# A branch over overflow code laid out in line, with a prefetch hint for TensorE, in a two-layer transformer trunk

## The chip, the cores and the metric

The kernel runs on one core of one Trainium2 chip. The metric is the device time of one execution in microseconds (us), as the median over several runs. The engines are TensorE (PE; its weight loads are PEld), VectorE (DVE), ScalarE (ACT), GpSimd (POOL) and SyncE (SP, which issues the DMAs here). Each engine has a sequencer that reads its own list of instructions; where an engine's name ends in q (PEldq, DVEq, SPq) the row is about the sequencer's own instructions, such as branches and DMA issues.

## The reference

A decoder trunk of two layers over 256 tokens of width 1024: in each, three parallel token mixers with a gated merge, then a layer of 16 experts with top-2 routing, each followed by a layer norm. What matters here is the expert layer:

```python
def moe_ffn(h, router_w, router_b, w1, w3, w2):
    hf = h.reshape(B * S, D)
    aff = jax.nn.sigmoid((hf @ router_w).astype(jnp.float32))
    ...
    combine = jnp.einsum('tk,tke->te', gate, jax.nn.one_hot(eidx, N_EXPERTS, dtype=jnp.float32)).astype(h.dtype)
    y = jnp.zeros_like(hf)
    for e in range(N_EXPERTS):
        y = y + combine[:, e:e + 1] * ((jax.nn.silu(hf @ w1[e]) * (hf @ w3[e])) @ w2[e])
    return y.reshape(B, S, D)
```

Every token goes to two of the 16 experts; w1 and w3 are 1024x512 and w2 is 512x1024 for each expert, in float32.

## The kernel before, in words

All weights are streamed from HBM in tiles of 1 MB (`wt`), each by one DMA that SP issues as soon as a buffer is free (`load`, L100). A layer runs its mixers first and then the experts.

The experts are taken in 8 pairs, p = 0 to 7, with room for CAP = 64 tokens for each expert. For one pair TensorE multiplies the gathered tokens `xe` with w1 and w3 (`up`, matmul L1557: 64 matmuls over 8 weight tiles), VectorE and ScalarE make the gated hidden value (`hidden`, L1567 to L1569), TensorE transposes it (`turn`, L1575), and multiplies it with w2 (`down`, L1600: 32 matmuls over 4 weight tiles). `combine` (L1515 in layer 0, L1520 in layer 1) adds the result, weighted, to the sums `z` or `y`. The order of the blocks on TensorE is written out by hand: `block()` issues each behind the one before it (the list `PEQ`). From p = 1 on the down-projection of pair p - 1 runs behind the up-projection of pair p; at p = 3 and p = 7 the pair's own down-projection follows at once.

An expert may be given more than 64 tokens. For that case there is `overflow()` (L1449 to L1497), once in each layer, behind the combine of pair 3. It loads the largest count of any expert into a register of every engine (`values_load`, L1452) and branches on it (`tc.If`, L1453). The body is four nested loops (L1468) that compute the experts' products over all 256 tokens for those beyond 64. With these inputs no expert has more than 64 tokens, so the body never runs: every engine goes from L1453 to whatever follows the body, on TensorE the up-projection of pair 4.

How the two ways out of L1453 are laid out in the instruction lists is set by the argument `preferred_fallthrough_block`. Before, it is False: behind the conditional branch stands the block for "no overflow", which holds a semaphore instruction and an unconditional branch that jumps over the overflow code.

```python
over = nc.values_load(mxi[0:1, 0:1], min_val=0, max_val=S)
with tc.If(over > CAP, preferred_fallthrough_block=False):
```

Of the kernel before, what the change touches and what calls it, by code (L numbers as in the profile page):

```python
# [25 lines left out]
CAP = 64  # L26
# [43 lines left out]
def trunk(ctx, tc, x, consts, pcol, rowv, gb, wfm, wng, wdv, wmla, wcmp, wcmp2, wu, wbr, wout, rw, mw1, mw3, mw2, out):  # L70
# [252 lines left out]
    def ln_cols(i, c):  # L323
        g0, b0 = PC_LN + 16 * i, PC_LN + 16 * i + 8
        return pc[:, g0 + c:g0 + c + 1], pc[:, b0 + c:b0 + c + 1]
# [1008 lines left out]
    def moe(l, R):  # L1334
# [93 lines left out]
        def affine():  # L1428
            w = load_gb(mh, 1 + 2 * l, "gt1", nc.sync)
            for j, op in enumerate((ALU.mult, ALU.add)):  # L1430
                for t in range(2):
                    V.tensor_tensor(out=res[:, t], in0=res[:, t], in1=w[:, j * D:j * D + D], op=op)
# [16 lines left out]
        def overflow():  # L1449
            V.tensor_scalar(wov, rks, float(CAP), None, op0=ALU.is_gt)  # L1450
            V.tensor_mul(wov, wov, cb)
            over = nc.values_load(mxi[0:1, 0:1], min_val=0, max_val=S)  # L1452
            with tc.If(over > CAP, preferred_fallthrough_block=False):  # L1453
                hx = mx[0].tile([P, 4, S], F32, name="hx", tag="xe0")
                hy = [gp.tile([P, 2, S], F32, name="hy", tag="yh") for _ in range(2)]
                hT = [hx[:, k] for k in range(4)] + [hy[k // 2][:, k % 2] for k in range(4)]
                for k in range(KD):
                    ps = pf.tile([P, S], F32, name="pt")
                    for t in range(2):
                        for j, src in enumerate((hhi, hlo)):  # L1460
                            T.matmul(ps, src(t, k)[:, 0], idb[:, P - P * t:3 * P - P * t],
                                     start=(t == 0 and j == 0), stop=(t == 1 and j == 1))
                    g, b = ln_cols(1 + 2 * l, k)
                    V.tensor_scalar(hT[k], ps, g, b, op0=ALU.mult, op1=ALU.add)
                up_w = [src[l].rearrange("q e p (k j h f c) -> q e p k j h f c", k=2, j=2, h=2, f=2) for src in (mw1, mw3)]
                down_w = mw2[l].rearrange("q c h p (f j o) -> q c h p f j o", f=2, j=2)
                wv = wov.rearrange("p t (q j) -> p t q j", j=2)
                with tc.For_i(0, E // 2, 1) as q, tc.For_i(0, 2, 1) as j, tc.For_i(0, 2, 1) as h, tc.For_i(0, 2, 1) as f:  # L1468
                    wc = gp.tile([P, 2], F32, name="wc")
                    V.tensor_copy(wc, wv[:, :, ds(q, 1), ds(j, 1)].rearrange("p t o a -> p (t o a)"))  # L1470
                    gf = gp.tile([P, S], F32, name="gf", tag="g")
                    pp = []
                    for src in up_w:
                        ps = pf.tile([P, S], F32, name="pt")
                        for e in range(4):
                            w = gp.tile([P, 2, P], F32, name="fa", tag="yl")
                            G.dma_start(w, src[ds(q, 1), e, :, :, ds(j, 1), ds(h, 1), ds(f, 1)].rearrange(
                                "a p k b d g c -> (a b d g p) k c"))
                            for k in range(2):
                                T.matmul(ps, w[:, k], hT[2 * e + k], start=(e == 0 and k == 0), stop=(e == 3 and k == 1))  # L1480
                        pp.append(ps)
                    A.activation(gf, pp[0], AF.Tanh, scale=0.5)
                    V.scalar_tensor_tensor(gf, gf, 1.0, pp[0], op0=ALU.add, op1=ALU.mult)
                    V.scalar_tensor_tensor(gf, gf, 0.5, pp[1], op0=ALU.mult, op1=ALU.mult)
                    for c in range(2):
                        w2 = gp.tile([P, 512], F32, name="fc", tag="yl")
                        G.dma_start(w2, down_w[ds(q, 1), c, ds(h, 1), :, ds(f, 1), ds(j, 1)].rearrange("a g p b d o -> (a g b d p) o"))
                        for t in range(2):
                            ps = pf.tile([P, 512], F32, name="pt")
                            T.matmul(ps, gf[:, t * P:(t + 1) * P], w2, start=True, stop=True)  # L1490
                            tm = gp.tile([P, 512], F32, name="tm", tag="g")
                            V.tensor_scalar(tm, ps, wc[:, t:t + 1], None, op0=ALU.mult)
                            if last:
                                T.matmul(ya[t][c], ident, tm, start=False, stop=False, skip_group_check=True)
                            for k in () if last else range(4):
                                T.matmul(ya[2 * c + k // 2][:, k % 2, t * P:(t + 1) * P], tm[:, k * P:(k + 1) * P], ident,
                                         start=False, stop=False, skip_group_check=True)  # L1497
# [48 lines left out]
        def block(f, *a):  # L1546
            with tc.issue_after(PEQ[-1]) if PEQ else nullcontext():
                i = f(*a)
            PEQ.append(getattr(i, "ins", i))
# [15 lines left out]
        def hidden(p, h1, h3):  # L1565
            g = gp.tile([P, FF], F32, name="g")
            A.activation(g, h1, AF.Tanh, scale=0.5)  # L1567
            V.scalar_tensor_tensor(g, g, 1.0, h1, op0=ALU.add, op1=ALU.mult)  # L1568
            V.scalar_tensor_tensor(g, g, wsl[:, p:p + 1], h3, op0=ALU.mult, op1=ALU.mult)  # L1569
            return g  # L1570
# [45 lines left out]
        for p in range(8):  # L1616
            hs = [pf.tile([P, FF], F32, name="pt") for _ in range(2)]
            for nm, hh in zip(("w1", "w3"), hs):
                block(up, p, nm, hh)
            if p == 0:  # L1620
                lent.close()
                mx.append(right.enter_context(tc.tile_pool(name="mx2", bufs=1, side="right", reuse_waits="tile")))
                gp = right.enter_context(tc.tile_pool(name="gp", bufs=2, side="right", reuse_waits="tile"))
                block(slot_weights, 0)
            g = hidden(p, *hs)
            if p in (0, 4):
                block(gather, p // 2 + 1)
                block(slot_weights, p // 2 + 1)
                block(slots_T, p)
                block(turn, p, g)  # L1630
                if p == 4 and last:
                    affine()
                continue
            block(down, p - 1)
            block(turn, p, g)
            block(slots_T, p)
            if p == 2:
                block(gather, 2)
                block(slot_weights, 2)
            if p == 7 and not last:  # L1640
                pool, tag = X0["zf"] = ST.take()
                Z["zf"] = pool.tile([P, KD, S], F32, name="zf", tag=tag)
                for k in range(KD):
                    block(residual, k)
            for c in range(2):
                block(combine, p - 1, c)
            if p in (3, 7):
                block(down, p)
            if p == 3:
                for c in range(2):  # L1650
                    block(combine, 3, c)
                overflow()
                PEQ.clear()
# [45 lines left out]
    for l in range(L):  # L1699
        rt, z, zf = moe(l, mixer(l, rt, z, zf))  # L1700
# [128 lines left out]
```

## Time and profile before

| | us |
|---|---|
| median of 3 runs | 1056.8 (1055.84 to 1057.39) |
| the profiled execution | 1058.08 |
| its span in the trace | 1056.4 |
| TensorE busy | 1012.6 (96% of the span) |
| VectorE busy | 533.9 (51%) |
| ScalarE busy | 424.0 (40%) |
| GpSimd busy | 31.8 (3%) |
| mean granted TensorE clock | 0.98 of full speed |

The span is what the rows below are timed in: their starts count from its beginning. The profiled execution's own time is 1.7 us longer than its span, and 1.3 us longer than the median of the three runs shown. Busy time counts the engine's own operations; branches, semaphore instructions and DMA issues are not counted in it.

### The profile page before, as it was taken

What the parts mean: (1) busy time and instruction counts of PE and PEld (TensorE: products, weight loads), DVE (VectorE), ACT (ScalarE), POOL (GpSimd) and SP (SyncE); (2) the same over time, 40 slices, a digit from 0 to 9 for tenths busy, and PEclk for the clock granted to TensorE, in tenths of its full rate; (3) what the DMA queues carried; (4) which work ended last, traced back from release to release, by engine and by line L of the source; (5) the groups of instructions that cost most, each with busy time, mean ns of one, the idle gap of its engine ahead of it and who ended that gap; (6) DMA issues with size and microseconds to landing.
All of it is one profiled execution on the core that took longest, in us unless ns stands there. A gap on an engine that the chain in (4) does not pass through costs nothing. (4 is left out here: it accounts for less than half of the span.)

```text
span 1056.4 us, 16800 instructions
## 1 busy us (share of the span) xinstructions
PE 1012.6 (96%) x6498; PEld 711.9 (67%) x6498; DVE 533.9 (51%) x1493; ACT 424.0 (40%) x991; POOL 31.8 (3%) x46
## 2 busy tenths in 40 slices
PE   8999999999999997999999999999999999979994
PEld 7888988999864343433587888799998544424332
DVE  7745778785762121211285558777777422102315
ACT  6563777555321021100465537855553221101111
POOL 0300000000000000000002001000000000000001
PEclk9999999999999998999989999999999999989997
DMA  9664335448777999999846534335497789999992
GB/s 356 253 231 150 121 121 180 164 157 358 297 272 317 421 421 420 420 421 420 294 176 218 187 125 157 145 135 181 162 381 282 284 327 421 421 419 420 420 420 92
DMA packets 45546, 294.91 MB, mean 279 GB/s; under 512 B 5137, under 2 KB 7953, under 8 KB 11793
## 3 DMA queue, kind: packets, MB, share of 16 engines
q1 hardware_dynamic: 44880, 291.51, 70.5%
q10 hardware_dynamic: 576, 2.24, 0.6%
q8 instruction: 53, 0.87, 0.3%
q14 instruction: 37, 0.30, 0.1%
HBM read 292.68 MB, written 1.05 MB: 278 GB/s over the span
## 5 line engine op out<-in xcount | busy, mean ns | idle before, releaser
L1557 PE MATMUL pt<-wt,xe 128*64 128x512 f32 x1024 | 229.0, 604 | 12.7 <-issue 12.6
L371 DVE TENSOR_TENSOR wlo<-wt,whi 128x1024 fp32r<-128x1024 f32 (+4 forms) x146 | 167.5, 1149 | 83.1 <-ACT whi L370 77.0
L370 ACT CAST whi<-wt 128x1024 fp32r<-128x1024 f32 (+4 forms) x146 | 143.8, 987 | 148.3 <-PE acc L376 106.2
L1557 PEld LDWEIGHTS pt<-wt,xe 128*64 128x64 f32 x1024 | 73.4, 139 | 153.5 <-issue 149.2
L375 PE MATMUL acc<-hi,whi 128*128 128x256 f32 x576 | 165.3, 288 | 1.7 <-ACT whi L370 0.8
L377 PE MATMUL acc<-hi,wlo 128*128 128x256 f32 x576 | 164.0, 286 | 0.9 <-DVE wlo L371 0.9
L376 PE MATMUL acc<-lo,whi 128*128 128x256 f32 x576 | 162.4, 282 | 0.0
L1600 PE MATMUL pt<-wt,gT 128*64 128x512 f32 (+1 forms) x544 | 113.7, 568 | 0.0
L375 PEld LDWEIGHTS acc<-hi,whi 128*128 128x128 f32 x576 | 108.2, 188 | 7.9 <-issue 3.9
L377 PEld LDWEIGHTS acc<-hi,wlo 128*128 128x128 f32 x576 | 108.3, 188 | 4.3 <-DVE wlo L371 2.1
L376 PEld LDWEIGHTS acc<-lo,whi 128*128 128x128 f32 x576 | 108.7, 189 | 0.3 <-DVE lo L339 0.2
L1609 ACT CAST yh<-pt 128x512 fp32r<-128x512 f32 (+1 forms) x34 | 19.1, 561 | 184.0 <-PE pt L1600 184.0
L1600 PEld LDWEIGHTS pt<-wt,gT 128*64 128x64 f32 x544 | 38.8, 137 | 70.3 <-issue 66.1
L1568 DVE SCALAR_TENSOR_TENSOR g<-g,pt 128x512 f32<-128x512 f32 x16 | 11.0, 686 | 136.7 <-ACT g L1567 136.7
L1610 DVE TENSOR_TENSOR yl<-pt,yh 128x512 fp32r<-128x512 f32 (+1 forms) x34 | 22.4, 660 | 105.8 <-ACT yh L1609 103.1
L1567 ACT ACTIVATE g<-pt 128x512 f32<-128x512 f32 x16 | 9.6, 597 | 130.5 <-PE pt L1557 130.5
L375 PE MATMUL acc<-ob,whi 128*128 128x256 f32 x192 | 56.8, 296 | 1.1 <-DVE gt L892 0.8
L376 PE MATMUL acc<-ob,whi 128*128 128x256 f32 x192 | 54.2, 282 | 0.0
L377 PE MATMUL acc<-ob,wlo 128*128 128x256 f32 x192 | 54.1, 284 | 0.0
L1569 DVE SCALAR_TENSOR_TENSOR g<-g,wsl,pt 128x512 f32<-128x512 f32 x16 | 11.9, 747 | 69.0 <-PE pt L1557 69.0
L1382 ACT ACTIVATE xe<-pt,pc 128x128 f32<-128x128 f32 x60 | 24.2, 454 | 55.8 <-PE pt L1324 53.9
L659 DVE COPY ts<-pt 128x384 f32<-128x384 f32 x56 | 30.6, 553 | 30.7 <-PE pt L628 30.6
(399 smaller groups left out, 1773.4 us busy)
## 6 DMA issues: line engine op xcount, KB each, us to landing
wt<-in_mw SPq DMA_DIRECT2D x190, 1024.0 KB, 15.6
wt<-in_wfm SPq DMA_DIRECT2D x38, 1024.0 KB, 4.9
wt<-in_wbr SPq DMA_DIRECT2D x12, 1024.0 KB, 4.8
wt<-in_wcmp SPq DMA_DIRECT2D x8, 1024.0 KB, 6.2
wt<-in_wout SPq DMA_DIRECT2D x8, 1024.0 KB, 8.2
wt<-in_wdv SPq DMA_DIRECT2D x4, 1024.0 KB, 6.4
wt<-in_wmla SPq DMA_DIRECT2D x4, 832.0 KB, 5.2
wt<-in_wng SPq DMA_DIRECT2D x4, 560.0 KB, 10.6
```

The costliest lines, as they stand in the source:

```text
L370: X["hi"] = A.copy(hi, src).ins
L371: X["lo"] = V.tensor_sub(lo, src, hi.bitcast(F32)).ins
L375: T.matmul(ps, a[0], b[0], start=start, stop=False)
L376: T.matmul(ps, a[0], b[1], start=False, stop=False)
L377: return T.matmul(ps, a[1], b[0], start=False, stop=stop)
L659: X["ts"] = V.tensor_copy(ts, pt).ins
L1382: A.activation(x[:, k], pj, AF.Identity, bias=bb, scale=g)
L1557: i = T.matmul(hh[64 * j:64 * j + 64], xe[p][:, 2 * h + k, j * CAP:(j + 1) * CAP], wt[:, c0:c0 + FF], start=(h == 0 and k == 0), stop=(h = ...
L1569: V.scalar_tensor_tensor(g, g, wsl[:, p:p + 1], h3, op0=ALU.mult, op1=ALU.mult)
L1600: i = T.matmul(v[64 * j:64 * j + 64], gT[:, 2 * h + f, 64 * j:64 * j + 64], w2t[:, c0 + ks[0] * P:c0 + ks[1] * P], start=(h == 0 and f == ...
L1609: X0["yh"] = A.copy(yh[:, d], v).ins
L1610: V.tensor_sub(yl[:, d], v, yh[:, d].bitcast(F32))
```

## The change

It has two parts. The branch of L1453 is laid out the other way: the overflow code now follows the conditional branch directly, and the branch itself, taken, jumps over it. And ahead of the last down-projection before that branch, at p == 3, the program asks for a branch hint on TensorE that marks this branch, by its label, as likely taken. Both happen once in each layer.

```diff
-            with tc.If(over > CAP, preferred_fallthrough_block=False):
+            with tc.If(over > CAP, preferred_fallthrough_block=True, label="ov"):
...
             for c in range(2):
                 block(combine, p - 1, c)
+            if p == 3:
+                tc.mark_branch_hint_location('ov', 'LikelyTaken', engines=[mybir.EngineType.PE])
             if p in (3, 7):
                 block(down, p)
             if p == 3:
```

Two lines are added ahead of L1646, so later lines count two more in the changed kernel (L1825 becomes L1827).

TensorE's list around the branch in layer 0, where L1461 is the first matmul of the overflow code, reads:

```order
@@ -1877,5 +1878,4 @@
 L1452 TENSOR_LOAD mxi
 L1453 COMPARE_AND_BRANCH
-L1453 UNCONDITIONAL_BRANCH
 L1461 MATMUL pt<-idb,yh 128x256
 L1461 MATMUL pt<-idb,yl 128x256
```

The unconditional branch that stood between the conditional one and the overflow code is gone from there.

At the other end of the overflow code of layer 0, where its loops (L1468) close and the up-projection of pair 4 (L1557) begins, TensorE's list reads:

```order
@@ -1947,4 +1947,6 @@
 L1468 COMPARE_AND_BRANCH
 L1468 UNCONDITIONAL_BRANCH
+L1453 UNCONDITIONAL_BRANCH
+L1827 BRANCH_PREFETCH_HINT
 L1557 MATMUL pt<-wt,xe 64x512 x32
 L1324 MATMUL pt<-SS,yh 128x256
```

The "no overflow" block's branch now stands behind the overflow code, where it jumps to the next instruction and so has nothing to skip. Behind it stands a hint, ahead of everything else that TensorE does up to the next branch: it is the one for layer 1.

The hint for layer 0 stands at the start of TensorE's whole list, ahead of the warm-up matmuls on `junk`:

```order
@@ -1,4 +1,5 @@
-L1825 UNCONDITIONAL_BRANCH
-L1686 MATMUL pt<-junk 128x256 x3
+L1827 UNCONDITIONAL_BRANCH
+L1827 BRANCH_PREFETCH_HINT
+L1688 MATMUL pt<-junk 128x256 x3
 L291 MATMUL pt<-idf,r 128x128 x12
 L964 MATMUL acc<-z,gl 128x258 x10
```

So neither hint stands where the source line does, ahead of the last down-projection: the scheduler has moved both to the head of the straight piece of code that ends in the branch. Apart from these rows TensorE's list is the same as before, row for row. On the other engines the same unconditional branch moves behind the overflow code, and nothing else changes; they get no hint.

## Rows read from the trace of the kernel before

**Rows 1.** Busy time of each engine, whole span: us, share, instructions.
```profile
PE 1012.6 (96%) x6498; PEld 711.9 (67%) x6498; DVE 533.9 (51%) x1493; ACT 424.0 (40%) x991; POOL 31.8 (3%) x46
```

**Rows 2.** TensorE's waits, whole span: line waited for: us in total, times, longest.
```profile
PE pt L1557 <- issue: 12.6, 2, 6.4
PE acc L964 <- DVE z L298: 2.3, 2, 1.8
```

**Rows 3.** Chain that ended last, 930 to 1030 us: start us, us, what.
```profile
933.31 6.08 issue
939.39 16.88 PE pt L1557 x64
...
961.35 13.88 PE pt L1557 x64
...
975.23 6.87 PE pt L1600 x32
```

**Rows 4.** Line L1453, layer 0: engine op xcount: ns min/median/max, first to last start.
```profile
L1453 DVEq COMPARE_BRANCH  x2: 51/56/60, 412.6 to 412.8; - x2
L1453 PEldq COMPARE_BRANCH  x2: 98/3076/6053, 413.3 to 413.8; - x2
L1453 SPq COMPARE_BRANCH  x2: 38/46/53, 414.8 to 414.9; - x2
```

**Rows 5.** Line L1453, layer 1, the same columns.
```profile
L1453 PEldq COMPARE_BRANCH  x2: 81/2954/5827, 932.9 to 933.4; - x2
```

**Rows 6.** Timeline of TensorE: start, us, instruction xcount, [idle before <- releaser].
```profile
413.37 0.28 PE L1515 MATMUL z<-CT,yl 128*128 128x256 f32 x1
420.06 15.43 PE L1557 MATMUL pt<-wt,xe 128*64 128x512 f32 x64 [6.41 <-issue]
...
961.28 13.95 PE L1557 MATMUL pt<-wt,xe 128*64 128x512 f32 x64
```

**Rows 7.** Windows: us, busy PE PEld DVE ACT POOL, PEclk, DMA share, GB/s.
```profile
420.00:423.30 3.30, 3.24 (x9) 1.12 (x11) 0.00 (x0) 0.00 (x0) 0.00 (x0) 0.53 1.04 427
939.30:943.00 3.70, 3.61 (x10) 1.28 (x12) 0.00 (x0) 0.00 (x0) 0.00 (x0) 0.50 1.02 418
943.00:946.00 3.00, 3.00 (x12) 0.93 (x10) 0.00 (x0) 0.00 (x0) 0.00 (x0) 0.61 0.99 410
946.00:950.00 4.00, 4.00 (x20) 1.38 (x18) 0.00 (x0) 0.57 (x1) 0.00 (x0) 1.00 1.01 420
```

**Rows 8.** DMA queues: whole span, then 384 to 413, then 413.8 to 420: packets, MB, share.
```profile
q8 instruction: 53, 0.87, 0.3%
...
q8 instruction: 1, 0.02, 0.2%
...
q8 instruction: 1, 0.02, 1.1%
```

**Rows 9.** Timeline of SP, one weight tile late in each layer's experts.
```profile
476.98 0.33 SPq L100 DMA_DIRECT2D wt<-in_mw  x1
...
1003.82 0.33 SPq L100 DMA_DIRECT2D wt<-in_mw  x1
```

**Rows 10.** DMA issues of 476 to 478, and of 1003 to 1005 alike: KB, us to landing.
```profile
wt<-in_mw SPq DMA_DIRECT2D x1, 1024.0 KB, 19.8
```

**Rows 11.** Timeline of TensorE, the down-projections that use those two tiles.
```profile
501.25 7.04 PE L1600 MATMUL pt<-wt,gT 128*64 128x512 f32 x32
...
1021.91 7.04 PE L1600 MATMUL pt<-wt,gT 128*64 128x512 f32 x32
```

**Rows 12.** Windows as in rows 7, in layer 1's experts and behind layer 0's.
```profile
980.00:1000.00 20.00, 20.00 (x96) 7.71 (x94) 6.75 (x8) 2.04 (x4) 0.00 (x0) 1.00 1.01 420
520.00:540.00 20.00, 16.61 (x103) 14.09 (x100) 15.43 (x27) 10.38 (x18) 0.00 (x0) 0.83 0.55 189
```

**Rows 13.** SP's waits, 934 to 1020 us, columns as in rows 2.
```profile
SPq L100 <- DMA wt<-in_mw: 35.8, 19, 2.1
```

## The prediction

> **What bounds the kernel now.** I read the busy times first: TensorE works 96% of the span, no other engine more than 67% [rows 1]. So only what TensorE waits for can be gained, and its list of waits comes next [rows 2]. Almost all of it is one line: 12.6 us in two waits, ahead of the up-projection at L1557, put down to "issue", which means that no data was late. The next wait in the list is 2.3 us in all. The chain that ended last holds the second of the two as a piece of its own, 6.08 us from 933.31 [rows 3], so it is paid in full.
>
> What the engine does in them is told by line L1453. In layer 0 TensorE's sequencer has two branches there, 98 ns and 6053 ns long [rows 4]. The short one starts at 413.3; the long one starts at 413.8 and ends at 419.85, and TensorE, whose last matmul ended at 413.65, starts again at 420.06 after 6.41 us of idling [rows 6]. By the order of the list the long one is the unconditional branch over the overflow code. Layer 1 repeats it: 81 and 5827 ns [rows 5]. The same pair takes 60 ns at most on VectorE and 53 ns on SyncE [rows 4]. So a jump as such is cheap; what is slow is TensorE getting at its code on the other side. The queue that carries instructions shows this: 53 packets for 0.87 MB in the whole run, 16.4 KB each; one in the 29 us ahead of the jump, and one more in the 6.2 us of the jump itself [rows 8]. I read this as the packet with the up-projection of pair 4 being asked for when the jump is taken, and not before.
>
> A second cost hangs on the first. [...] The 64 matmuls of that up-projection take 15.43 us in layer 0 and 16.88 us in layer 1 [rows 3, 6], against 13.95 for the next pair's [rows 6]. That is 1.48 and 2.93 us.
>
> **The change, part by part.** *The jump.* The unconditional branch of 6.05 and 5.83 us leaves TensorE's path; the conditional branch becomes the taken jump. Its price where its target is already there is not in the trace on TensorE. Bounds: below, SyncE's 38 ns; above, the 6.05 us of a jump whose target is not there [rows 4]. If the hint does what its name says, the nearest rows are TensorE's own conditional branch, 81 and 98 ns, and I take 0.15 us. That leaves a gain of 6.05 - 0.15 = 5.90 us in layer 0 and 5.83 - 0.15 = 5.68 us in layer 1 [rows 4, 5].
>
> *The clock.* With an idle time of well under a microsecond I expect no fall, so 1.48 and 2.93 us come back as well. Layer 0 can gain 5.90 + 1.48 = 7.4 us, layer 1 5.68 + 2.93 = 8.6 us.
>
> *What is late next.* TensorE, coming sooner, may run into its weights. In layer 0 the tightest tile is issued at 476.98 and lands 19.8 us later, at 496.8 [rows 9, 10]. It is the last of the four tiles of the down-projection that starts at 501.25 [rows 11], so 24 of 32 matmuls come first, at 6.87 / 32 = 0.215 us each [rows 3]: needed at 506.4. The slack of 9.6 us is over 7.4, so all of layer 0's gain passes. Behind it the DMAs are at 0.55 of their capacity [rows 12] and the mixers follow whenever TensorE does.
>
> Layer 1 is another matter. The last tile of the same kind is issued at 1003.82 and lands at 1023.62, and is needed at 1021.91 + 24 x 0.215 = 1027.07 [rows 9 to 11]: 3.4 us of slack. It can't land sooner because TensorE is sooner: the DMAs are at 1.01 of capacity and 420 GB/s [rows 12], SP itself waits 35.8 us for earlier transfers [rows 13], and a tile of 1024 KB at 420 GB/s takes 2.5 us where TensorE uses one up in 8 x 0.215 = 1.72 us. So the gain of layer 1 is cut from 8.6 to 3.4 us, and 5.2 us of it turn into waits for weights near the end.
>
> *The hints.* Two instructions on TensorE's sequencer. No row of before shows one; the nearest are its short branches of 81 and 98 ns [rows 4, 5]. I take 0.05 us on the path for each, 0.1 us in all. The first stands at the start, where TensorE waits for `junk` anyway; the second right behind the layer-0 jump. Below, they cost nothing. What one costs at worst is a rival. The other engines' jumps are off the path: they end by 414.9 [rows 4], while SyncE works transfers ahead and the others have nothing to do.
>
> *The sum.* 7.4 + 3.4 - 0.1 = 10.7 us. Against the profiled execution, 1058.08 us, that is 1047.4. This execution was 1.28 us over the median of the runs, so against the median, 1056.8, I predict **1046.1 us**.
>
> Below that: layer 0 could give all 6.41 + 1.48 = 7.89 us (0.5 more), the hints nothing (0.1), and the runs of before reach 1.0 under their median: 1044.5. Above: layer 0 keeps its slow start (1.5 more), and the runs reach 0.6 above: 1048.3.
>
> [...] The trace shows one packet fetched in the jump and a 6.05 us jump [rows 4, 8]. [...]
>
> **The rivals.**
> 1. *Layer 1's cap costs more than the gain that it cuts.* TensorE that waits for each tile is busy 1.72 of 2.5 us, and the clock may fall again; at half speed a tile takes 3.44 us, longer than its transfer, and the lead is lost. It recovers as soon as weights pile up, so at worst the 3.4 us of layer 1 are gone: 1049.5. For: the clock fell after each pause. Against: it stayed at 0.83 with TensorE busy 16.61 of 20 us [rows 12]. Chance 0.10.
> 2. *The change doesn't do what it says: the hint is spent or ignored.* The hints stand at 0 and at 420 us and their branches at 413.3 and 932.9 [rows 4 to 6], over 410 us later each. At 53 packets in 1056 us, some 20 packets of ordinary code come in between [rows 8]. If the code fetched for the hint gives way to them, or the hint holds for what comes next only, the 6 us move from the unconditional to the conditional branch, and only a short branch goes: 1056.7. [...] Against: the hint names its branch by label, and so can be held until that branch is near. Chance 0.17.
> 3. *Only one of the two jumps is served.* Layer 0 alone gives 1056.8 - 7.4 = 1049.4, layer 1 alone 1056.8 - 3.4 = 1053.4. For: the two hints stand behind different things, the program's start and a jump. Chance 0.05.
> 4. *Slower: the hint is obeyed at once.* It fetches its target when it is read and takes the place of the packet that TensorE needs next. TensorE then waits for that one as it waits in the jump, 6.0 us, and pays 1.5 us of slow clock: 7.4 us for a hint, and the jumps stay as they are. With one hint 1064.2, with both 1071.6. It decides whether a packet of the instruction queue comes right behind each hint and TensorE idles on "issue" there. [...] Against: a prefetch that stops the code being run would be of no use. Chance 0.08.
>
> **How the numbers follow.** The forecast has 0.60. Its own range is 1044.5 to 1048.3. With rival 1 (up to 1049.5) and rival 3 that is 0.75 for faster by more than 0.2%, about what a measurement of this kernel can tell from no change (2.1 us). Rival 2 is the 0.17 for the same, rival 4 the 0.08 for slower. To hold 8 in 10 the range must reach rival 2, at most 1056.7 and half a microsecond of spread: 1044.5 to 1057.2.
>
> **What would show it.** Right: TensorE's branch at L1453 takes 0.1 to 0.2 us in both layers; the waits on "issue" at L1557 are gone; the 64 matmuls behind it take 13.95 us at a clock of 1.0; an instruction packet arrives ahead of the branch; and in layer 1 TensorE waits for `wt` at L1557 and L1600 in the last 40 us, about 5 us in all. Wrong: a branch of some 6 us at L1453, now the conditional one (rival 2 or 3), an "issue" wait at the start or behind L1453 of layer 0 (rival 4), or a clock under 1.0 between 1000 and 1040 us (rival 1). If layer 1's weights landed sooner than now, the cap would be wrong and the time under 1044.

## The result: 1045.5 us, 1.1% faster, through another wait than forecast in layer 1

The changed kernel takes 1045.47 us (median of 4 runs, 1043.64 to 1046.80), the kernel before 1056.32 us (4 runs, 1055.61 to 1057.39). The ratio is 0.9891, with a 95% interval of 0.9879 to 0.9902. The forecast was 1046.1 us. One execution below, the profiled one of hint_late, was disturbed (1263.5 us at a mean clock of 0.748): its time is left out, and only the order of its events is read.

The profiled execution took 1044.16 us, with a span of 1042.5 us, 13.9 us under that of before. The busy line of its page answers to [rows 1]:

```profile
PE 1005.7 (96%) x6498; PEld 707.3 (68%) x6498; DVE 533.7 (51%) x1493; ACT 423.7 (41%) x991; POOL 31.7 (3%) x46
```

TensorE does the same 6498 matmuls in 6.9 us less busy time: the rest of the gain is idle time. The busy part I put down to the clock (mean granted clock 0.980 before, 0.989 now). Its waits over the whole span, as in [rows 2], now begin with:

```profile
PE pt L1557 <- DVEq L1453: 4.7, 1, 4.7
PE acc L964 <- DVE z L298: 1.8, 1, 1.8
```

Two waits of 6.4 and 6.2 us on "issue" have become one of 4.7 us, for VectorE's sequencer at the branch. Line L1453 in layer 0, then in layer 1 (engine, operation, count: ns min/median/max, first to last start; [rows 4, 5] of before):

```profile
L1453 DVEq COMPARE_BRANCH  x1: 72/72/72, 411.1 to 411.1; - x1
L1453 DVEq EVENT_SEMAPHORE  x1: 21/21/21, 411.7 to 411.7; - x1
L1453 PEldq COMPARE_BRANCH  x1: 384/384/384, 411.9 to 411.9; - x1
...
L1453 DVEq COMPARE_BRANCH  x1: 63/63/63, 920.9 to 920.9; - x1
L1453 PEldq COMPARE_BRANCH  x1: 365/365/365, 921.7 to 921.7; - x1
L1453 PEldq EVENT_SEMAPHORE  x1: 51/51/51, 922.1 to 922.1; - x1
L1453 DVEq EVENT_SEMAPHORE  x1: 21/21/21, 926.6 to 926.6; - x1
```

TensorE's jump, 6053 and 5827 ns before, takes 384 and 365 ns. But in layer 1 VectorE's semaphore instruction, which belongs to the "no overflow" block, comes 5.7 us behind VectorE's branch, and TensorE waits for it. In layer 0 it comes after 0.6 us. The up-projection behind the branch in TensorE's timeline ([rows 6]), and the windows of the same stretches (columns of [rows 7]), the last one to be set beside [rows 12]:

```profile
412.72 13.95 PE L1557 MATMUL pt<-wt,xe 128*64 128x512 f32 x64 [0.48 <-PEq L1453]
...
926.64 15.65 PE L1557 MATMUL pt<-wt,xe 128*64 128x512 f32 x64 [4.65 <-DVEq L1453]
```

```profile
412.72:416.00 3.28, 3.28 (x16) 1.40 (x18) 0.00 (x0) 0.00 (x0) 0.00 (x0) 1.00 1.03 417
926.60:930.40 3.80, 3.76 (x10) 1.17 (x12) 0.00 (x0) 0.00 (x0) 0.00 (x0) 0.57 1.02 418
930.40:934.00 3.60, 3.60 (x20) 1.19 (x18) 0.00 (x0) 0.00 (x0) 0.00 (x0) 0.98 1.00 416
980.00:1000.00 20.00, 20.00 (x96) 7.71 (x94) 5.73 (x7) 2.03 (x4) 0.00 (x0) 1.00 1.01 422
```

In layer 0 the granted clock is 1.00 behind an idle time of 0.48 us, and the 64 matmuls take 13.95 us. In layer 1, behind the wait of 4.65 us, it is 0.57 for 3.8 us, and the 64 take 15.65 us.

**Where the 13.9 us went.** I set the same matmul of both executions side by side. Ahead of the branch in layer 0 the new one leads by 1.4 us. Behind the 64 matmuls it leads by 435.49 - 426.67 = 8.8 us, so layer 0 gave 7.4. From the branch of layer 1 (lead 932.9 - 921.7 = 11.2) to the end of its 64 matmuls (956.27 - 942.29 = 14.0) layer 1 gave 2.8. That is 10.2 us at the changed places. The other 3.7 us lie elsewhere, most of them in three stretches of mixer code that ran at a granted clock of 0.51 to 0.69 in the one profile and of 1.00 in the other. The windows of before, then of the changed kernel:

```profile
297.20:302.00 4.80, 4.80 (x23) 4.80 (x23) 3.75 (x25) 2.14 (x4) 0.00 (x0) 0.69 0.80 292
533.00:537.00 4.00, 4.00 (x26) 4.00 (x26) 4.00 (x8) 0.00 (x0) 0.00 (x0) 0.66 0.88 340
819.00:822.50 3.50, 3.50 (x14) 3.50 (x12) 3.33 (x23) 2.15 (x4) 0.00 (x0) 0.51 0.77 253
```

```profile
296.80:300.00 3.20, 3.20 (x21) 3.20 (x21) 2.96 (x19) 2.15 (x4) 0.00 (x0) 1.00 0.63 210
524.40:527.00 2.60, 2.60 (x25) 2.60 (x25) 2.60 (x5) 0.00 (x0) 0.00 (x0) 1.00 0.94 306
809.00:811.50 2.50, 2.50 (x16) 2.50 (x16) 2.33 (x14) 1.80 (x4) 0.00 (x0) 1.00 0.69 187
```

In the profiles of the experiments below the matmuls at L1315, which lie in the first and the third of these stretches, have a median of 334 ns or of 520 to 525 ns, with or without hints (layout_only 334 in layer 0 and 522 in layer 1, hint_pe_dve 334 and 525, hint_l1_only 525 and 522), so I do not count them for the change. Single runs of one kernel differ by 3 us, and a profile must be compared stage by stage.

### The profile page after: what moved, and what is told of

Same layout as the page of the kernel before. It is cut to its first block, busy times and chain, and to the rows that moved or that the text cites. A ratio compares the mean times of both kernels' runs of the same rounds, so it can differ in the third digit from the quotient of the medians.

```text
span 1042.5 us, 16792 instructions
## 1 busy us (share of the span) xinstructions
PE 1005.7 (96%) x6498; PEld 707.3 (68%) x6498; DVE 533.7 (51%) x1493; ACT 423.7 (41%) x991; POOL 31.7 (3%) x46
## 5 line engine op out<-in xcount | busy, mean ns | idle before, releaser
L1557 PE MATMUL pt<-wt,xe 128*64 128x512 f32 x1024 | 226.3, 598 | 5.3 <-DVEq L1453 4.7
L1557 PEld LDWEIGHTS pt<-wt,xe 128*64 128x64 f32 x1024 | 72.9, 138 | 143.9 <-issue 133.7
```

The source lines that it names most:

```text
L1557: i = T.matmul(hh[64 * j:64 * j + 64], xe[p][:, 2 * h + k, j * CAP:(j + 1) * CAP], wt[:, c0:c0 + FF], start=(h == 0 and k == 0), stop=(h = ...
```

## The experiments

**Is it the layout or the hint?** First the hints are taken away and the layout is kept (every diff here is against the changed kernel).

```diff
-            if p == 3:
-                tc.mark_branch_hint_location('ov', 'LikelyTaken', engines=[mybir.EngineType.PE])
```

> The changed kernel without its two hints; the overflow code stays in line behind the branch. If the hint is what serves the jump: TensorE's branch at L1453, now the taken conditional one, takes about 6 us in both layers, the 64 matmuls behind it run at half clock again, and the time is that of the kernel before, 1055 to 1057 us. If the layout does it (one branch in place of two): the branch takes 0.4 us, as in the changed kernel, and the time is 1044 to 1047 us.

Measured: 1055.17 us (12 runs, 1053.84 to 1056.59; ratio 0.998, 0.9971 to 0.9988). Its line L1453 over both layers, and its instruction queue over the whole span:

```profile
L1453 PEldq COMPARE_BRANCH  x2: 327/3169/6011, 411.7 to 931.0; - x2
L1453 PEldq EVENT_SEMAPHORE  x2: 51/51/51, 417.8 to 931.3; - x2
```

```profile
q8 instruction: 53, 0.87, 0.3%
```

In layer 0 the conditional branch now holds the whole jump, 6.01 us. In layer 1 the branch took 0.33 us, and TensorE idled for 5.8 us right behind its semaphore instruction: there the stall came one instruction later. Both jumps cost about what they did. The layout alone is worth 0.2%; nearly all of the gain is the hint's.

Then the hints are kept and the layout of before is put back.

```diff
-            with tc.If(over > CAP, preferred_fallthrough_block=True, label="ov"):
+            with tc.If(over > CAP, preferred_fallthrough_block=False, label="ov"):
```

> The layout of before (the unconditional branch ahead of the overflow code does the jump) with the hints of the changed kernel, which now name a conditional branch that is not taken. If the hint serves only the branch that it names, the jump still takes about 6 us and the time is that of before, 1055 to 1058 us. If the code fetched for the wrong target also displaces the code that TensorE needs, it is slower, 1058 to 1066 us. If the hint serves whatever jump comes next, the layout was not needed: 1044 to 1047 us.

Measured: 1056.71 us (10 runs; ratio 1.0003, 0.9991 to 1.0014). The same line:

```profile
L1453 PEldq COMPARE_BRANCH  x4: 90/2976/5978, 411.6 to 930.9; - x4
```

A hint that names a branch which is not taken changed nothing that these runs can tell, neither way. So both parts are needed, the layout (1055.17 us by itself) and the hint (1056.71 by itself): the layout makes the named branch the one that jumps, and with the hint that jump takes 0.37 to 0.38 us in the changed kernel.

**How far ahead must the hint be read?** In the changed kernel the hints are read at 0.9 and 412.5 us, 411 and 509 us ahead of their branches. Three kernels hold them to a place in TensorE's order: behind the combine of pair 2, where the source line stands; behind the down-projection of pair 3; and behind the combine of pair 3. The first of them reads:

```diff
             if p == 3:
-                tc.mark_branch_hint_location('ov', 'LikelyTaken', engines=[mybir.EngineType.PE])
+                with tc.issue_after(PEQ[-1]):
+                    tc.mark_branch_hint_location('ov', 'LikelyTaken', engines=[mybir.EngineType.PE])
```

> The changed kernel with both hints held to the place where its source has them: behind the combine of pair 2, ahead of the down-projection of pair 3, some 9 us ahead of the branch (at about 403 us in layer 0) in place of 410 to 510 us. In the changed kernel one instruction packet came at 386 us, ahead of the branch, and none when the hint itself was read, at 0.9 us. If the hint only decides what that packet fetches (the jump's target in place of the next code in sequence), it comes too late here: branch of about 6 us, 1054 to 1057 us. If the hint makes a fetch of its own once its branch is near, 9 us are more than the 6 us of a jump: the branch takes 0.4 us, a packet more comes between 403 and 412 us, and the time is 1044 to 1047 us.

> The hints are held still later, behind the down-projection of pair 3, some 2.3 us ahead of the branch (at about 409.6 us, branch at 411.9). With the hints 13 us ahead, an instruction packet began 3.8 us behind each hint, beside the one in sequence. If a hint read late makes a fetch of its own, the packet begins at about 413.4 and is there at 414.5 to 415.5: the branch takes 2.5 to 3.6 us in layer 0, half of before, and the time is 1047 to 1051 us (TensorE's 4.7 us wait for VectorE in layer 1 covers the same stall there). If a hint must be read ahead of the packet in sequence, or a full 6 us ahead, the branch takes about 6 us and the time is 1052 to 1057 us.

> The hints are held to the last place ahead of the branch: behind the combine of pair 3, just ahead of the load of the count. Behind the down-projection the hint was read 6.4 us ahead of the branch, its packet began 3.4 us later, and the branch still took only 0.44 us. Here the lead is some 1 to 2.5 us. If a hint only starts the fetch sooner, what is left of the 6 us jump is 6 less the lead: the branch takes 3 to 5 us in layer 0, an idle time ahead of L1557 of the same length, and the time is 1047 to 1052 us. If a hint read that late does nothing, the branch takes 6 us: 1051 to 1056 us. If the lead does not matter: 0.4 us and 1044 to 1047 us.

Measured: hint_late 1044.96 us (5 runs, 1044.20 to 1046.61), hint_later 1046.75 (4 runs, 1044.08 to 1048.94), hint_last 1056.31 (10 runs, 1053.74 to 1058.95). The branches over both layers, of hint_late, and the hints and branches of hint_later and of hint_last:

```profile
L1453 PEldq COMPARE_BRANCH  x2: 384/413/442, 492.4 to 1112.5; - x2
```

```profile
L1827 PEldq BRANCH_PREFETCH_HINT  x2: 36/40/45, 405.5 to 915.5; - x2
...
L1453 PEldq COMPARE_BRANCH  x2: 443/465/487, 411.9 to 921.8; - x2
```

```profile
L1827 PEldq BRANCH_PREFETCH_HINT  x2: 41/43/45, 411.3 to 929.9; - x2
...
L1453 PEldq COMPARE_BRANCH  x2: 6101/6140/6179, 412.0 to 930.5; - x2
```

With 411 or 509 us, with 13 us (in hint_late's profile, hint read at 479.5 and branch at 492.4) and with 6.4 us of lead the jump takes 0.37 to 0.49 us; with 0.6 to 0.7 us it takes all of its 6.1 us, and nothing is saved. My expectation for hint_later was wrong in its lead: I put the hint 2.3 us ahead, by the place of the matmuls around it, but the sequencer read it at 405.5, while TensorE was still at the down-projection ahead of it in the list (402.8 to 409.9 us in the changed kernel). What lies between was not tried.

When packets come on the instruction queue (q8) differs with the lead. In hint_later one came between the hint and the branch (window 405.5 to 411.9, the row below), and in hint_late one between 483 and 485 us, behind the hint at 479.5 and ahead of the branch at 492.4. In hint_last none came from 390 to 412 us, up to the branch.

```profile
q8 instruction: 1, 0.02, 1.1%
```

In the changed kernel the page has 51 packets, two fewer than before ([rows 8]):

```profile
q8 instruction: 51, 0.84, 0.3%
```

None comes in the first 24 us, where the first hint is read; one comes at 386.3 us, 25.6 us ahead of the branch, as one did before (387.8, 25.5 us ahead). In the kernel before two come within 10 us of TensorE's slow jump in each layer, at 417.4 and 423.2 us and at 936.8 and 942.6, which is 3.6 and 9.4, then 3.4 and 9.2 us behind its start. In the changed kernel one comes within 10 us of each branch, at 415.6 and 925.4 us, 3.7 us behind it; in layer 0 TensorE, at work from 412.72 to 426.67, does not wait for it. So in the changed kernel one packet fewer comes in that time in each layer. Which code a packet holds no row shows, and so these runs do not show by what way a hint serves its jump.

**What is each layer's hint worth?** The hint is asked for `if p == 3 and not last`, or `and last`.

> The changed kernel with layer 0's hint alone. By the terms of the sum, layer 0 gives about 7.4 us and layer 1's share of the result is 1.4 us of idle time and 1.2 us of clock: 1047.5 to 1049.5 us, with TensorE stalling some 6 us at or behind L1453 in layer 1. If VectorE's late semaphore in layer 1 (5.7 us behind its branch) already costs as much as TensorE's own jump, layer 1's hint is worth nothing: 1045 to 1047 us.

> The changed kernel with layer 1's hint alone, the last of four: no hint gave 1055.2 us, layer 0's alone 1047.8, both 1045.5. If the two layers add up, layer 1's hint is worth 2.3 us and layer 0's jump costs 6 us again: 1052 to 1054 us. VectorE's semaphore in layer 1 was late (5.5 to 5.7 us behind its branch) in every kernel with a hint on TensorE in that layer and none on VectorE, and quick (0.5 us) in both kernels without a hint there; if that is what goes with it, it is late here too and TensorE waits 4 to 5 us for it at L1557. If it takes both hints, VectorE is quick here, TensorE does not wait, and layer 1 gains up to the weights' cap: 1050 to 1052 us.

Measured: layer 0 alone 1047.79 us (4 runs), layer 1 alone 1055.06 us (11 runs, 1051.49 to 1056.11). TensorE's longest waits of the two:

```profile
PE pt L1557 <- PEq L1453: 6.4, 2, 6.0
```

```profile
PE pt L1557 <- PEq L1453: 6.1, 1, 6.1
PE pt L1557 <- DVEq L1453: 4.5, 1, 4.5
```

Layer 0's hint is worth 1055.17 - 1047.79 = 7.4 us against layout_only. Layer 1's is worth 2.3 us beside layer 0's (1047.79 - 1045.47) and 0.1 us without it, where I had expected 2.3: how far the two differ can't be told from runs of one kernel that spread over 2 to 5 us. In both cases with a hint in layer 1, TensorE's wait of some 6 us is replaced by one of 4.5 to 4.7 us for VectorE's late semaphore, which takes most of the gain back.

**What holds layer 1 now?** VectorE gets the same hint.

```diff
-                tc.mark_branch_hint_location('ov', 'LikelyTaken', engines=[mybir.EngineType.PE])
+                tc.mark_branch_hint_location('ov', 'LikelyTaken', engines=[mybir.EngineType.PE, mybir.EngineType.DVE])
```

> The changed kernel with the same hint on VectorE too. In the changed kernel TensorE waits 4.7 us at L1557 in layer 1 for a semaphore that VectorE gives only after its own jump, 5.7 us behind its branch. If that jump is a fetch like TensorE's, VectorE's semaphore comes 0.6 us behind its branch in layer 1 as in layer 0, TensorE's wait and the slow clock behind it go (4.7 + 1.7 us), but the weights cap what is left: the last tiles landed 1.0 to 1.5 us ahead of their use, so the time falls by 1.0 to 1.5 us only, to 1042.5 to 1045.5. If the weights do not cap, 6.4 us are gained: 1038 to 1040. If the wait is for something else, nothing changes: 1044 to 1047.

Measured: 1045.22 us (5 runs, 1043.24 to 1045.93), 0.25 us under the changed kernel and level with it within the spread. Line L1453 on VectorE in layer 1, then TensorE's waits from 915 us to the end, one window, and two rows of its timeline:

```profile
L1453 DVEq COMPARE_BRANCH  x1: 74/74/74, 923.2 to 923.2; - x1
L1453 DVEq EVENT_SEMAPHORE  x1: 21/21/21, 923.8 to 923.8; - x1
```

```profile
PE pt L1600 <- DMA wt<-in_mw: 2.2, 4, 0.6
PE pt L1557 <- DMA wt<-in_mw: 1.5, 3, 0.6
```

```profile
995.00:1015.00 20.00, 16.26 (x72) 4.34 (x68) 2.13 (x3) 1.18 (x2) 0.00 (x0) 1.00 1.01 421
```

```profile
1002.36 1.94 PE L1557 MATMUL pt<-wt,xe 128*64 128x512 f32 x8 [0.56 <-DMA wt<-in_mw]
1004.84 1.94 PE L1557 MATMUL pt<-wt,xe 128*64 128x512 f32 x8 [0.54 <-DMA wt<-in_mw]
```

VectorE's semaphore comes 0.6 us behind its branch, TensorE's 4.65 us are gone, and 3.7 us of waits for weight tiles stand at the end in their place. From TensorE's branch of layer 1 to the end of the span it takes 120.2 us, against 120.8 without VectorE's hint; before it was 1056.4 - 932.9 = 123.5 us. Up to the end of the 64 matmuls behind the branch VectorE's hint gains 6.0 us, and 5.4 of them are lost again: from 999.9 us on TensorE begins the 8 matmuls of a tile every 2.5 us (rows above), seven times, in place of every 1.72 us, which is 5.3 us. To show that the tiles are the cap, their loads are halved late in layer 1, without and with VectorE's hint (`n` is the tile's width in the load; the matmuls' columns are taken modulo 1024 there):

```diff
-            key, src, n = item
+            (key, src, n), late = item, {"w1": 5, "w3": 5, "w2": 10}
...
-                parts = 2 if key[1:] == ("q", 0) else 1
+                parts, n = 2 if key[1:] == ("q", 0) else 1, n // 2 if key[0] == 1 and key[1] in late and key[2] >= late[key[1]] else n
```

> The changed kernel, but from pair 5 of layer 1 on only half of each weight tile is loaded, and that half is used twice (the other half of these weights is left out; one tile, the very last, is still loaded whole). The DMAs have time to spare there. In the changed kernel no tile is late, since VectorE's jump holds TensorE 4.7 us: so no change from it, 1044 to 1047 us. If weights do set its end, it is faster by more than 1.5 us.

> The same halved loads with the hint on VectorE too. With whole tiles this hint took 4.7 us of waiting and the slow clock away from layer 1, and 3.7 us came back as waits for weight tiles, so the time stayed at 1045.2 us. If the weights are the cap: no wait for tiles here and 3 to 5.5 us faster than the kernel with halved loads and TensorE's hints alone, 1040 to 1042.5 us. If the end is set by something else, it stays at 1044 to 1046 us.

Measured: 1049.06 us without VectorE's hint and 1042.92 us with it (4 runs each), 6.1 us apart; both lie above their forecasts, the second by 0.4 us. TensorE's waits from 915 us to the end, of the first and of the second:

```profile
PE pt L1557 <- DVEq L1453: 4.6, 1, 4.6
PE y L1520 <- DVE r L1532: 1.4, 1, 1.4
```

```profile
PE y L1520 <- DVE r L1532: 1.4, 1, 1.4
PE y L1520 <- DVE yl L1610: 1.0, 1, 1.0
```

No wait for a tile is left in either. From TensorE's branch of layer 1 to the end the first takes 1049.7 - 926.1 = 123.6 us, the second 1041.1 - 924.0 = 117.1: with weights in time VectorE's hint is worth 6.5 us, with whole tiles 0.6. That the first is not level with the changed kernel, as I had expected, has two causes in its profile: it is 4.4 us behind already at the start of pair 4's up-projection and 4.8 at its end, ahead of any halved tile, which I put down to clock in the mixers (at L1315 a median of 520 and 522 ns in its two layers, 334 in both in the changed kernel); and both halved kernels lose some 2 us in the two waits at L1520, one behind the down-projection of pair 4 (1.0) and one at the very end (1.4), where the blocks come in another order.

**Is there more to be had?** Everything that has to do with the overflow case is left out (`overflow()` is not called).

> The overflow code, the load of the count and the branch are left out on all engines, and with them the hints. This is the most that any serving of the jump can give. If the weights cap layer 1: within 1 us of the kernel with hints on TensorE and VectorE, 1042 to 1045 us, with TensorE waiting for weight tiles in the last 40 us. If they do not cap: about 1038 us.

Measured: 1045.71 us (5 runs, 1045.38 to 1048.35), no faster than the changed kernel; by the median it is 0.7 us above the forecast with a cap. From 915 us on, its first wait is for tiles:

```profile
PE pt L1600 <- DMA wt<-in_mw: 1.9, 4, 0.5
```

So nothing is left that another treatment of the branch would be seen to give back while the tiles are the cap. (Without the branch the scheduler also mixes pair 4's up-projection with the combine of pair 3, so this is the same amount of work in a slightly other order.) No kernel with the whole computation was clear of the changed one.

**Why is VectorE late in layer 1 alone?** One more kernel has a TensorE list that is a warm-up matmul shorter (`range(NW0 - 1)`).

> The changed kernel with two warm-up matmuls on junk in place of three. VectorE's list is unchanged. Its jump in layer 1 was slow (semaphore 5.5 to 5.7 us behind the branch) in every kernel that has both hints on TensorE and none on VectorE, and quick (0.5 us) with none or one, although VectorE's own list is the same in all of them; TensorE's list is two, one or no instruction longer. If what decides is where VectorE's code comes to lie when TensorE's list changes its length, the four instructions less make VectorE's jump in layer 1 quick, and TensorE's 4.7 us wait goes: TensorE waits for weights there, 1043.5 to 1046.5 us. If it is TensorE's own fetch that holds VectorE's, the semaphore stays 5.5 us late and the wait stays: 1044 to 1047.5 us. Only the trace tells them apart, since the weights cap what layer 1 can gain.

Measured: 1045.35 us (4 runs), VectorE's semaphore at 926.4 behind a branch at 920.7, and TensorE's wait still 4.7 us. So a shift of TensorE's code by these four instructions does not make VectorE quick; that another shift would is not excluded. What the runs have in common is this: VectorE's semaphore comes 5.4 to 5.7 us behind its branch in layer 1 in all kernels of the new layout with a hint on TensorE in that layer and none on VectorE (also in hint_last, where TensorE's hint was of no use), and 0.5 us behind it in layout_only and hint_l0_only, which have no hint there. The second instruction queue (q14, 36 packets of 8 KB in the changed kernel) has packets in that time, though its rows name no engine: in the changed kernel they come 3.0, 3.7 and 6.7 us behind VectorE's branch in layer 0 (at 414.1, 414.8 and 417.8 us), and 2.9, 3.7, 6.8 and 9.0 us behind it in layer 1 (at 923.8, 924.6, 927.7 and 929.9). Whose instructions they are no row shows. That the late semaphore goes with VectorE's own instructions being late is my reading; hint_pe_dve agrees, where a hint on VectorE brings the semaphore 0.6 us behind its branch. Why VectorE is late there as soon as TensorE has a hint in that layer is open.

## Why the prediction was right, and where it was not

The result lies 0.6 us from the forecast, and the sum of 10.7 us compares with 10.85 between the medians; read from the two profiles at the changed places it is 10.2 us. Layer 0 came out as worked out, layer 1 near its number for another reason. By the steps:

- *The jump.* I took 0.15 us for a served jump; it took 0.37 and 0.38. The idle time ahead of L1557 in layer 0 went from 6.41 to 0.48 us, 5.93 against 5.90 forecast: the jump was dearer by 0.23 us, but the idle time before was 0.36 us longer than the jump itself, and most of that went too.
- *The clock.* In layer 0 1.48 us came back, as forecast (13.95 for 15.43), at a granted clock of 1.00 where [rows 7] have 0.53. In layer 1 only 1.2 of 2.9 us came back, with a wait of 4.65 us left and a clock of 0.57 behind it.
- *Layer 0's weights.* All of its 7.4 us passed; hint_l0_only, 7.4 us under layout_only, agrees.
- *Layer 1.* Forecast 3.4 us, capped by weights, with about 5 us of waits for tiles. The stages give 2.8 us, and there is no wait for a tile in the changed kernel. **The step that failed is the sentence that the other engines' jumps are off the path.** Its rows are those of layer 0, and it held for the layout of before: there VectorE's semaphore instruction stood between the conditional branch and the jump, as its rows of line L1453 in layer 1 show (last one below), so a slow jump of VectorE's would have kept nobody waiting there. The new layout puts that semaphore behind the jump, where it comes at 926.6 us, and TensorE, no longer late itself (its branch starts at 921.7 and takes 0.37 us), meets it. I listed the cost of the moved branch on the other engines at nothing, and had not asked which of their instructions moves to the far side of the jump with it. In the kernel before:

```profile
L1453 DVEq COMPARE_BRANCH  x2: 47/51/55, 932.1 to 932.5; - x2
L1453 DVEq EVENT_SEMAPHORE  x1: 21/21/21, 932.5 to 932.5; - x1
```

- *The cap itself* is real, and hidden behind that wait: once VectorE is served, layer 1 gains 123.5 - 120.2 = 3.3 us, against 3.4 forecast, and 5.4 us are lost to the tiles, against 5.2 forecast; with halved loads the waits for tiles are gone and VectorE's hint gains 6.5 us. That VectorE's wait leaves 2.8 us and the cap 3.3 is chance, and it is why the total fits.
- *The upper end of the range* adds up to 1046.1 + 1.5 + 0.6 = 1048.2 us; 1048.3 is a slip of 0.1.
- *Rival 1*, a clock that falls while TensorE waits for tiles, is out: at 16.26 of 20 us busy the granted clock was 1.00 in hint_pe_dve. My ground against it was misread: 0.83 in [rows 12] is a mean over a stretch in which the clock did fall (0.66 from 533 to 537 us, in the windows above). *Rival 2*, a hint spent over 410 us, is out, too: the lead of 509 us served as well as that of 6.4. *Rival 3* is out, since both jumps were served; its two cases were built as kernels: layer 0 alone 1047.8 (forecast 1049.4), layer 1 alone 1055.1 (forecast 1053.4). *Rival 4*, a hint that is obeyed at once and starves TensorE, is out: no packet comes in the first 24 us, where a hint is read at 0.9, the list of TensorE's waits has none on "issue" in the changed kernel, nor in hint_later, where a packet follows the hint, and a hint on a branch that was not taken left the time as it was (ratio 1.0003).

## What to carry to other kernels

An idle engine whose wait behind a branch is put down to "issue" may be waiting for its own instructions, as I read it here (6.41 us of idle time before, 0.48 with the hint): look at the length of its branches and at the instruction queue, and let the branch that will be taken be the one that a hint names. A lead of 6.4 us was enough here, one of 0.7 us was not. Before a branch is laid out in another way, list what every engine does behind the jump that others wait for: a semaphore that moves to the far side can make that engine's delay everybody's (4.65 us of TensorE here). And when a stall is taken out of a stage whose transfers run at full rate (1.01 of capacity in [rows 12]), expect no more from it than the slack of its tightest tile (3.4 us by its rows here, 3.3 gained).

## What I had not expected of the hardware

- The hint may stand very early: read 411 and 509 us ahead of its branch it served as well as 6.4 us ahead, and at 0.6 to 0.7 us it did nothing at all (6.10 and 6.18 us).
- TensorE's sequencer read a hint that stands behind a 7 us down-projection while that was still at work (402.8 to 409.9 us in the changed kernel), at 405.5 us for a branch at 411.9.
- Short stretches of the mixers ran at a granted clock of 1.00 in one profile and of 0.51 to 0.69 in another of nearly the same code. The 16 matmuls at L1315 in layer 1 started between 808.6 and 811.3 us in the changed kernel, with a median of 334 ns, and between 818.6 and 822.8 with 525 ns in the kernel before; hint_l0_only had them quick there (334 ns) and slow in layer 0 (522), layout_only the other way round (522 and 334). Three such stretches make up most of 3.7 us between the two profiles, a third of what the change gives.
